# One written-out order of loads and stores on a single DMA queue, with six buffers and equal tiles

## The chip, the cores and the metric

One core of one Trainium2 chip. The metric is the device time of one execution in microseconds (us). "Span" is the length of the profiled execution, some 2 us shorter than the time.

A ratio below is the mean time of one kernel's runs over the mean time of the runs of the kernel before in the same rounds, so it is not quite the ratio of the medians that stand beside it. The batches of runs did not all go to the same chip, and the kernel before had a median between 239.82 and 240.45 us in them; so kernels of different batches are compared by their ratios.

## The reference

```python
# x: (16, 3, 512, 512) float32, factor = 1.5
mean = np.mean(x, axis=(2, 3), keepdims=True)
return np.clip(mean + factor * (x - mean), 0, 1)
```

There are 48 images of 1 MB. Each needs its mean before any of its pixels can be finished. 50.33 MB come in and 50.33 MB go out.

## The kernel before

A tile is four images: 128 partitions of 8192 numbers (32 KB a partition, 4.19 MB), 32 partitions to an image. The last four images are cut into two tiles of two images, whose rows are 16 KB.

```python
TILE_IMGS = [4] * 11 + [2, 2]
X_BUFS = 5
STORE_ENGINE = "gpsimd"
# ... (cut: constants, pools)
for i, N in enumerate(TILE_IMGS):
    # ... (cut: src and dst, rows of 32 KB or 16 KB, contiguous)
    nc.sync.dma_start(out=xt, in_=src)                       # load, SyncE's queue
    nc.vector.tensor_reduce(out=rsum, in_=xt, op=add)        # sums of rows
    nc.tensor.matmul(pbias, blockw[N], rsum)                 # sum over the image's partitions
    nc.scalar.copy(out=bias, in_=pbias)
    nc.scalar.activation(out=xt, in_=xt, func=Relu, bias=bias, scale=factor)
    nc.vector.tensor_scalar(out=xt, in0=xt, scalar1=1.0, op0=min)
    store_eng.dma_start(out=dst, in_=xt)                     # store, GpSimd's queue
```

Of the kernel before, what the change touches and what calls it, by code (L numbers as in the profile page):

```python
# [1 line left out]

# [4 lines left out]


TILE_IMGS = [4] * 11 + [2, 2]  # L10
X_BUFS = 5
STORE_ENGINE = "gpsimd"


@with_exitstack
def kernel(
    ctx: ExitStack,
    tc: tile.TileContext,
    x: bass.AP,
    factor: float,  # L20
    out: bass.AP,
):
    nc = tc.nc
    P = 128

    B, C, H, W = x.shape
    n_img = B * C
    n_pix = H * W

    factor = float(factor)  # L30
    f32 = mybir.dt.float32

    assert sum(TILE_IMGS) == n_img
    NMAX = max(TILE_IMGS)

    x_f = x.rearrange("b c h w -> (b c h w)")
    out_f = out.rearrange("b c h w -> (b c h w)")

    wconst = (1.0 - factor) / float(n_pix)

    consts = ctx.enter_context(tc.tile_pool(name="consts", bufs=1))
    blockw = {}
    for N in sorted(set(TILE_IMGS)):
        wt = consts.tile([P, P], f32, name=f"blockw{N}")
        PPI = P // N
        if N == 1:
            nc.gpsimd.memset(wt, wconst)
        else:
            nc.gpsimd.memset(wt, 0.0)  # L49
            for b in range(N):  # L50
                nc.gpsimd.memset(wt[b * PPI : (b + 1) * PPI, b * PPI : (b + 1) * PPI], wconst)  # L51
        blockw[N] = wt

    xpool = ctx.enter_context(tc.tile_pool(name="xpool", bufs=X_BUFS))
    rpool = ctx.enter_context(tc.tile_pool(name="rpool", bufs=12))
    bpool = ctx.enter_context(tc.tile_pool(name="bpool", bufs=12))
    psum = ctx.enter_context(tc.tile_pool(name="psum", bufs=8, space=bass.MemoryType.PSUM))

    if STORE_ENGINE == "sync":
        store_eng = nc.sync  # L60
    elif STORE_ENGINE == "act":
        store_eng = nc.scalar
    else:
        store_eng = nc.gpsimd

    pix_off = 0
    for i, N in enumerate(TILE_IMGS):
        FREE = n_pix * N // P
        npix_tile = n_pix * N

        xt = xpool.tile([P, NMAX * n_pix // P], f32, name="xt")[:, :FREE]
        src = bass.AP(tensor=x_f.tensor, offset=pix_off, ap=[[FREE, P], [1, FREE]])
        dst = bass.AP(tensor=out_f.tensor, offset=pix_off, ap=[[FREE, P], [1, FREE]])
        nc.sync.dma_start(out=xt, in_=src)  # L74

        rsum = rpool.tile([P, 1], f32)
        nc.vector.tensor_reduce(  # L77
            out=rsum,
            in_=xt,
            axis=mybir.AxisListType.X,  # L80
            op=mybir.AluOpType.add,
        )

        pbias = psum.tile([P, 1], f32)
        nc.tensor.matmul(pbias, blockw[N], rsum, start=True, stop=True)  # L85

        bias = bpool.tile([P, 1], f32)
        nc.scalar.copy(out=bias, in_=pbias)  # L88

        nc.scalar.activation(  # L90
            out=xt,
            in_=xt,
            func=mybir.ActivationFunctionType.Relu,
            bias=bias,
            scale=factor,
        )
        nc.vector.tensor_scalar(  # L97
            out=xt,
            in0=xt,
            scalar1=1.0,  # L100
            scalar2=None,
            op0=mybir.AluOpType.min,
        )
        store_eng.dma_start(out=dst, in_=xt)  # L104

        pix_off += npix_tile


# [1 line left out]
_INS = ['x', 'factor']  # L110
_OUTS = [((16, 3, 512, 512), 'float32')]
#: Inputs that are plain numbers.
_NUMBERS = {'factor': 1.5}


# [26 lines left out]
```

## Time and profile before

| | before |
|---|---|
| time, median | 240.48 us (240.43 to 240.62, 3 runs) |
| span | 238.6 us |
| bytes moved | 100.66 MB |
| VectorE, ScalarE busy | 66%, 37% |

From the page of the kernel before: the busy line, the row of DMA business (tenths, 40 equal slices of the span), the rate in the same slices, and the two queues with their packets, MB and share of the 16 DMA engines' time.

```profile
span 238.6 us, 238 instructions
PE 7.4 (3%) x26; PEld 6.5 (3%) x26; DVE 156.5 (66%) x26; ACT 89.1 (37%) x27; POOL 10.3 (4%) x25
...
DMA  7999999999999999999999999999999999999995
GB/s 269 434 439 439 439 439 352 439 434 439 439 439 439 439 434 434 423 428 412 423 439 439 434 439 439 439 439 439 434 428 426 426 404 428 431 434 439 428 434 214
...
q1 hardware_dynamic: 1872, 50.33, 49.4%
q0 software_dynamic: 1872, 50.33, 49.0%
```

The DMA engines are busy all the time and no computing engine is. Between the first and the last slice the rate is 439 GB/s or close to it, except at the seventh slice (352).

The windows view of the same run gives the rate in stretches of my choice. Its columns are the stretch, its length, the busy time of the five computing engines, the clock, the DMA share and the rate.

```profile
core 0: us, PE busy (x) PEld busy (x) DVE busy (x) ACT busy (x) POOL busy (x), PEclk, DMA share, GB/s
0.00:4.00 4.00, 0.00 (x0) 0.00 (x0) 0.00 (x0) 1.28 (x1) 1.26 (x12) 1.00 0.67 229
4.00:36.00 32.00, 1.14 (x4) 1.00 (x4) 21.96 (x4) 11.16 (x4) 0.00 (x0) 1.00 1.00 430
36.00:42.00 6.00, 0.00 (x0) 0.00 (x0) 6.00 (x1) 3.40 (x1) 0.67 (x1) 1.00 1.01 388
42.00:198.00 156.00, 5.18 (x18) 4.50 (x18) 112.47 (x19) 65.07 (x18) 4.80 (x9) 1.00 1.00 434
198.00:206.00 8.00, 0.56 (x2) 0.50 (x2) 7.66 (x3) 4.35 (x3) 0.69 (x1) 1.00 0.98 414
206.00:232.00 26.00, 0.56 (x2) 0.50 (x2) 8.37 (x3) 3.87 (x2) 2.84 (x3) 1.00 0.99 427
232.00:238.60 6.60, 0.00 (x0) 0.00 (x0) 0.00 (x0) 0.00 (x0) 0.00 (x0) 1.00 0.57 243
```

The view books a packet whole, so short stretches are coarse. The trace also has a record of every packet (start, duration, queue, size). Spread over their durations, these packets give 433 GB/s in the quiet stretches of this trace, loads alone (6 to 30 us), stores alone (210 to 224 us) or a mix; losses below are counted against 433.3. At that rate 100.66 MB need 232.3 us. The span has 6.3 us more: slow first packets (2.6 us lost before 4 us), the end (2.6 us after 232 us), a sag (a short stretch below the full rate, here 0.7 us) at 36 to 42 us, and 0.2 us with the 16 KB rows.

VectorE's two groups in the kernel before (line, engine, operation, operands, count | busy us, mean ns | idle us just before, and what ended it):

```profile
L77 DVE TENSOR_REDUCE rsum<-xt 128x1 f32<-128x8192 f32 (+1 forms) x13 | 104.4, 8029 | 61.7 <-DMA xt<-in_x_dram 61.7
L97 DVE TENSOR_SCALAR xt<-xt 128x8192 f32<-128x8192 f32 (+1 forms) x13 | 53.2, 4091 | 5.0 <-ACT xt L90 5.0
```

VectorE spends its idle time waiting for loads, 61.7 us in all: the computation keeps up.

### The profile page before, as it was taken

To read this page: it belongs to the slowest core of one execution; us is meant where nothing else is said; L and a number is where in the kernel's file an instruction comes from. 1 tells how busy PE (TensorE), PEld (TensorE's weight loads), DVE (VectorE), ACT (ScalarE), POOL (GpSimd) and SP (SyncE) were. 2 spreads that over 40 slices of the span, in tenths; PEclk is the share of its full clock that TensorE was granted. 3 is DMA by queue.
4 is the path that set the end of the run, shared out by engine and by line. 5 is a ranking of instruction groups with operands and counts; after the bars stand their busy time and mean duration, and the time that the engine had idled before them with its cause. 6 is when DMAs were issued, how large, how long until landed. Compare 5 with 4: busy or idle time off the path is not lost.

```text
span 238.6 us, 238 instructions
## 1 busy us (share of the span) xinstructions
PE 7.4 (3%) x26; PEld 6.5 (3%) x26; DVE 156.5 (66%) x26; ACT 89.1 (37%) x27; POOL 10.3 (4%) x25
## 2 busy tenths in 40 slices
PE   0000000000000000000000000000000000000000
PEld 0000000000000000000000000000000000000000
DVE  0088999999599079459629909917945979742300
ACT  2002966472906601900920650470190095406000
POOL 2000001000000000000000000000000000500000
DMA  7999999999999999999999999999999999999995
GB/s 269 434 439 439 439 439 352 439 434 439 439 439 439 439 434 434 423 428 412 423 439 439 434 439 439 439 439 439 434 428 426 426 404 428 431 434 439 428 434 214
DMA packets 3744, 100.66 MB, mean 422 GB/s; under 512 B 416, under 2 KB 416, under 8 KB 416
## 3 DMA queue, kind: packets, MB, share of 16 engines
q1 hardware_dynamic: 1872, 50.33, 49.4%
q0 software_dynamic: 1872, 50.33, 49.0%
HBM read 50.33 MB, written 50.33 MB: 422 GB/s over the span
## 4 chain that ended last, share of the span: by engine, by line
issue 38%; DMA 35%; DVE 18%; POOL 2%; POOLq 0%; SPq 0%
DMA xt<-in_x_dram 19%; DMA out_dram<-xt 16%; DVE rsum L77 11%; DVE xt L97 7%; POOL out_dram L104 2%; POOLq L137 0%; SPq L74 0%; POOLq L104 0%
## 5 line engine op out<-in xcount | busy, mean ns | idle before, releaser
L77 DVE TENSOR_REDUCE rsum<-xt 128x1 f32<-128x8192 f32 (+1 forms) x13 | 104.4, 8029 | 61.7 <-DMA xt<-in_x_dram 61.7
L90 ACT ACTIVATE xt<-xt,bias 128x8192 f32<-128x8192 f32 (+1 forms) x13 | 85.8, 6598 | 0.4
L97 DVE TENSOR_SCALAR xt<-xt 128x8192 f32<-128x8192 f32 (+1 forms) x13 | 53.2, 4091 | 5.0 <-ACT xt L90 5.0
L88 ACT COPY bias<-pbias 128x1 f32<-128x1 f32 x13 | 2.1, 160 | 130.6 <-PE pbias L85 130.6
L104 POOL DMA_DIRECT2D out_dram<-xt x13 | 9.0, 692 | 213.0 <-DVE xt L97 212.8
L85 PE MATMUL pbias<-rsum,blockw 128*128 128x1 f32 x26 | 7.4, 355 | 209.5 <-DVE rsum L77 209.5
L85 PEld LDWEIGHTS pbias<-rsum,blockw 128*128 128x128 f32 x26 | 6.5, 311 | 210.3 <-DVE rsum L77 107.1
L88 ACT ACT_TABLE_LOAD x1 | 1.3, 1283 | 0.8 <-PEq L123 0.8
L51 POOL MEMSET blockw<- 32x32 f32 (+1 forms) x6 | 0.8, 128 | 0.2
L49 POOL MEMSET blockw<- 128x128 f32 x2 | 0.3, 205 | 0.3 <-POOLq L123 0.3
L123 POOL MEMSET const-float32-0.0<- 128x1 f32 x1 | 0.1, 104 | 0.2 <-issue 0.2
L123 POOL MEMSET const-bfloat16-1.0<- 128x1 bf16 x1 | 0.1, 113 | 0.0
L123 POOL MEMSET const-uint8-127<- 128x1 uint8 x1 | 0.1, 113 | 0.0
L123 POOL MEMSET const-float32-1.0<- 128x1 f32 x1 | 0.1, 110 | 0.0
## 6 DMA issues: line engine op xcount, KB each, us to landing
xt<-in_x_dram SPq DMA_DIRECT2D x11, 4096.0 KB, 24.6
out_dram<-xt POOLq DMA_DIRECT2D x11, 4096.0 KB, 36.0
xt<-in_x_dram SPq DMA_DIRECT2D x2, 2048.0 KB, 19.5
out_dram<-xt POOLq DMA_DIRECT2D x2, 2048.0 KB, 19.1
```

The lines of the kernel that those rows point to most:

```text
L49: nc.gpsimd.memset(wt, 0.0)
L51: nc.gpsimd.memset(wt[b * PPI : (b + 1) * PPI, b * PPI : (b + 1) * PPI], wconst)
L77: nc.vector.tensor_reduce(out=rsum, in_=xt, axis=mybir.AxisListType.X, op=mybir.AluOpType.add,)
L85: nc.tensor.matmul(pbias, blockw[N], rsum, start=True, stop=True)
L88: nc.scalar.copy(out=bias, in_=pbias)
L90: nc.scalar.activation(out=xt, in_=xt, func=mybir.ActivationFunctionType.Relu, bias=bias, scale=factor,)
L97: nc.vector.tensor_scalar(out=xt, in0=xt, scalar1=1.0, scalar2=None, op0=mybir.AluOpType.min,)
L104: store_eng.dma_start(out=dst, in_=xt)
L123: nc = _bacc.Bacc("TRN2", target_bir_lowering=False, num_devices=1)
```

## The change

The intent: everything the DMA engines do is put into one queue in an order written out by hand, so that loads and stores take turns evenly; one more buffer; no half tiles. The core of the diff:

```diff
-TILE_IMGS = [4] * 11 + [2, 2]
-X_BUFS = 5
-STORE_ENGINE = "gpsimd"
+P = 128
+ROW = 8192
+BUFS = 6
 # ... (cut)
-    for i, N in enumerate(TILE_IMGS):
-        nc.sync.dma_start(out=xt, in_=src)
-        # ... (the same five operations)
-        store_eng.dma_start(out=dst, in_=xt)
+    def load(t):
+        xt = xpool.tile([P, ROW], f32, name="xt")
+        nc.sync.dma_start(out=xt, in_=dram(x_f, t))
+        tiles[t] = xt
+    def compute(t):
+        # ... (the same five operations)
+    def store(t):
+        nc.sync.dma_start(out=dram(out_f, t), in_=tiles.pop(t))
+    for t in range(min(BUFS, n_tiles)):
+        load(t)
+    for t in range(n_tiles):
+        compute(t)
+        store(t)
+        freed = t - 1
+        if 0 <= freed and freed + BUFS < n_tiles:
+            load(freed + BUFS)
```

On SyncE's queue this gives L0 to L5, S0, S1, L6, S2, L7, S3, L8, S4, L9, S5, L10, S6, L11, S7, S8, S9, S10, S11 (L is a load, S a store, tiles counted from 0).

More of the change, by code (lines that the diff above doesn't have):

```diff
@@ L5 @@
 import concourse.tile as tile
-from concourse import bass_utils, mybir
+from concourse import mybir
 from concourse._compat import with_exitstack
-TILE_IMGS = [4] * 11 + [2, 2]
-X_BUFS = 5
-STORE_ENGINE = "gpsimd"
+P = 128
+ROW = 8192
+BUFS = 6
 @with_exitstack
@@ L23 @@
     nc = tc.nc
-    P = 128
+    f32 = mybir.dt.float32
+    Alu = mybir.AluOpType
+    Act = mybir.ActivationFunctionType
     B, C, H, W = x.shape
-    n_img = B * C
-    n_pix = H * W
+    n_img, n_pix = B * C, H * W
+    ppi = n_pix // ROW
+    per_tile = P // ppi
+    n_tiles = n_img // per_tile
+    assert ppi * ROW == n_pix and per_tile * n_tiles == n_img
     factor = float(factor)
-    f32 = mybir.dt.float32
-    assert sum(TILE_IMGS) == n_img
-    NMAX = max(TILE_IMGS)
+    wconst = (1.0 - factor) / float(n_pix)
@@ L36, with dram @@
     x_f = x.rearrange("b c h w -> (b c h w)")
     out_f = out.rearrange("b c h w -> (b c h w)")
-    wconst = (1.0 - factor) / float(n_pix)
+    def dram(ap, t):
+        return bass.AP(tensor=ap.tensor, offset=t * P * ROW, ap=[[ROW, P], [1, ROW]])
     consts = ctx.enter_context(tc.tile_pool(name="consts", bufs=1))
-    blockw = {}
-    for N in sorted(set(TILE_IMGS)):
-        wt = consts.tile([P, P], f32, name=f"blockw{N}")
-        PPI = P // N
-        if N == 1:
-            nc.gpsimd.memset(wt, wconst)
-        else:
-            nc.gpsimd.memset(wt, 0.0)
-            for b in range(N):
-                nc.gpsimd.memset(wt[b * PPI : (b + 1) * PPI, b * PPI : (b + 1) * PPI], wconst)
-        blockw[N] = wt
@@ L54 @@
-    xpool = ctx.enter_context(tc.tile_pool(name="xpool", bufs=X_BUFS))
-    rpool = ctx.enter_context(tc.tile_pool(name="rpool", bufs=12))
-    bpool = ctx.enter_context(tc.tile_pool(name="bpool", bufs=12))
-    psum = ctx.enter_context(tc.tile_pool(name="psum", bufs=8, space=bass.MemoryType.PSUM))
-    if STORE_ENGINE == "sync":
-        store_eng = nc.sync
-    elif STORE_ENGINE == "act":
-        store_eng = nc.scalar
-    else:
-        store_eng = nc.gpsimd
-    pix_off = 0
-    for i, N in enumerate(TILE_IMGS):
-        FREE = n_pix * N // P
-        npix_tile = n_pix * N
-        xt = xpool.tile([P, NMAX * n_pix // P], f32, name="xt")[:, :FREE]
-        src = bass.AP(tensor=x_f.tensor, offset=pix_off, ap=[[FREE, P], [1, FREE]])
-        dst = bass.AP(tensor=out_f.tensor, offset=pix_off, ap=[[FREE, P], [1, FREE]])
-        nc.sync.dma_start(out=xt, in_=src)
-        rsum = rpool.tile([P, 1], f32)
-        nc.vector.tensor_reduce(
-            out=rsum,
-            in_=xt,
-            axis=mybir.AxisListType.X,
-            op=mybir.AluOpType.add,
-        )
-        pbias = psum.tile([P, 1], f32)
-        nc.tensor.matmul(pbias, blockw[N], rsum, start=True, stop=True)
-        bias = bpool.tile([P, 1], f32)
-        nc.scalar.copy(out=bias, in_=pbias)
-        nc.scalar.activation(
-            out=xt,
-            in_=xt,
-            func=mybir.ActivationFunctionType.Relu,
-            bias=bias,
-            scale=factor,
-        )
-        nc.vector.tensor_scalar(
-            out=xt,
-            in0=xt,
-            scalar1=1.0,
-            scalar2=None,
-            op0=mybir.AluOpType.min,
-        )
-        store_eng.dma_start(out=dst, in_=xt)
-        pix_off += npix_tile
@@ new lines @@
+    xpool = ctx.enter_context(tc.tile_pool(name="xpool", bufs=BUFS))
+    rpool = ctx.enter_context(tc.tile_pool(name="rpool", bufs=2))
+    bpool = ctx.enter_context(tc.tile_pool(name="bpool", bufs=2))
+    psum = ctx.enter_context(tc.tile_pool(name="psum", bufs=2, space=bass.MemoryType.PSUM))
+    blockw = consts.tile([P, P], f32, name="blockw")
+    nc.gpsimd.memset(blockw, 0.0)
+    for a in range(0, P, ppi):
+        nc.gpsimd.memset(blockw[a : a + ppi, a : a + ppi], wconst)
+    tiles = {}
@@ new lines, in load @@
+    def load(t):
[3 more added lines that the diff above has]
+    def compute(t):
+        xt = tiles[t]
+        rsum = rpool.tile([P, 1], f32, name="rsum")
+        nc.vector.tensor_reduce(out=rsum, in_=xt, axis=mybir.AxisListType.X, op=Alu.add)
+        pbias = psum.tile([P, 1], f32, name="pbias")
+        nc.tensor.matmul(pbias, blockw, rsum, start=True, stop=True)
+        bias = bpool.tile([P, 1], f32, name="bias")
+        nc.scalar.copy(out=bias, in_=pbias)
+        nc.scalar.activation(out=xt, in_=xt, func=Act.Relu, bias=bias, scale=factor)
+        nc.vector.tensor_scalar(out=xt, in0=xt, scalar1=1.0, scalar2=None, op0=Alu.min)
```

## The prediction

> **What bounds the kernel.** The data movement. The page gives 100.66 MB in a span of 238.6 us, with the DMA row at 9 tenths in 38 of 40 slices; VectorE is busy 66%, ScalarE 37%. The windows view gives 434 GB/s from 42 to 198 us with loads and stores mixed, and 430 from 4 to 36 us with loads alone; read packet by packet both are 433 GB/s (a 32 KB packet takes 1.213 us on one of 16 engines), and so is the stretch of stores alone (210 to 224 us). The rate does not depend on the mix of directions or the number of queues. The Trainium skill ("DMA: Bandwidth & Descriptors", section "Where 436 GB/s comes from") puts the ceiling at 435 GB/s, and its "Rules for kernel authors" say that spreading DMAs over issuing engines does not help bandwidth; the trace agrees with both.
>
> So the floor is 100.66 MB / 433 GB/s = 232.3 us. The span is 6.3 us above it. From the windows and packets: 0 to 4 us loses 2.6 us (first packet at 1.75 us, slow first packets); 232 to 238.6 us loses 2.6 us (engines finish from 235.1 to 236.8 us, then 1.8 us of completion); 36 to 42 us, at 388 GB/s, loses 0.7 us (the first GpSimd store is issued at 36.06 us, its first packet comes some 4.5 us later, and the load stream sags meanwhile); 198 to 206 us, at 414 GB/s, loses 0.2 us (16 KB rows of the last loads). The rest is noise.
>
> **What the change does.**
> - Stores move from GpSimd's software queue to SyncE's hardware queue: removes the sag, 0.7 us. GpSimd's issue (0.53 us, once 2.46 us) was hidden.
> - Equal tiles remove the 16 KB rows, 0.2 us. The last tile takes 8.7 + 0.6 + 0.2 + 7.1 + 4.4 us to compute, some 22 us, against 11 for a half, but its store has to queue behind others.
> - One FIFO with six buffers: loads 0 to 5 fill it to about 61 us; stores 0 and 1 are ready at 36 and 49 us. Load k waits on SyncE until store k-6 has landed, and holds back what follows. In slots of 9.7 us (4.19 MB at 433 GB/s): loads 0-5, store 0, store 1, load 6, store 2, load 7, ... load 11 in slot 18, stores 7-11 in slots 19-23. When load k is let go, 7 us or more of work is still queued, so the queue never runs dry. Load 11 lands near 187 us, is computed near 210, and its store's turn comes near 225. No compute comes on the path.
> - Reused DMA semaphores (eight in turn) belong to DMAs long done.
>
> Start and end stay.
>
> **Prediction.** 240.5 - 0.9, rounded: 239.5 us, range 238.4 to 240.6. Chances: faster by over 2% 3%, within 2% 94%, slower by over 2% 3%. A gain of 2% would need 4.8 of the 6.3 us above the floor, most of which the change doesn't touch.
>
> **What would show it.** Right: all slices at one rate from 4 us to the end, the slice at 36 us no longer at 352; one hardware queue with about 98% of the engines; SyncE's waits on stores long, yet no gap in the data. Wrong: drops in the GB/s row where loads and stores alternate; a VectorE wait in the chain near the end; the last stores starved.
>
> **What would make it wrong.** In one ring the completion write of a store may hold up the next load (in the tail of stores alone no such gap shows, so I doubt it); the engines may drift apart by more than the present 1.7 us; single-direction blocks may differ from a mix in HBM, which the two pure stretches speak against.

## The result and the profile after

| | before | after |
|---|---|---|
| time, median of 6 runs | 240.45 us (239.74 to 240.75) | 241.63 us (240.99 to 242.50) |
| ratio, 95% interval | | 1.0058 (1.0034 to 1.0083) |
| span of the profiled execution | 238.6 us | 240.7 us |

The kernel became slower by 0.6%: a small loss, clear of the noise, where a gain of 0.4% was predicted. Its runs also spread more, 1.5 us against 1.0. The profiled execution after the change is the slowest of the six (242.50 us), so the second trace below (run a1, 241.56 us) is used beside it.

The page after, the same lines, and the line of the chain that ended last by engine:

```profile
span 240.7 us, 227 instructions
...
DMA  7999999999899999999999999999999999999991
GB/s 272 425 436 436 436 436 436 436 436 430 359 436 436 436 430 430 436 436 436 436 436 430 436 436 436 436 436 430 436 430 436 414 436 430 436 430 430 436 425 71
...
q1 hardware_dynamic: 3456, 100.66, 97.6%
...
DVE 43%; ACT 21%; issue 17%; DMA 9%; PE 2%; SPq 0%; DVEq 0%
```

One queue has 97.6% of the engines' time. The sag did not go: it stands in the eleventh slice (359). The last slice moved only 71 GB/s, against 214 before. The windows view of the changed kernel (columns as before) shows the sag at 58 to 62 us, and the old loss at 198 to 206 us (16 KB rows) gone:

```profile
36.00:58.00 22.00, 0.98 (x4) 0.95 (x4) 22.00 (x4) 10.85 (x3) 0.00 (x0) 1.00 0.99 429
58.00:62.00 4.00, 0.14 (x1) 0.05 (x1) 4.00 (x2) 3.79 (x2) 0.00 (x0) 1.00 1.10 385
62.00:198.00 136.00, 3.90 (x14) 3.50 (x14) 91.82 (x15) 54.45 (x15) 0.00 (x0) 1.00 1.00 431
198.00:206.00 8.00, 0.00 (x0) 0.00 (x0) 8.00 (x2) 0.00 (x0) 0.00 (x0) 1.00 1.04 451
206.00:232.00 26.00, 0.56 (x2) 0.50 (x2) 8.36 (x2) 7.28 (x2) 0.00 (x0) 1.00 0.99 429
```

The end in slices of 1 us, from the windows views (columns as before), of the kernel before and then of the changed one:

```profile
237.00:238.00 1.00, 0.00 (x0) 0.00 (x0) 0.00 (x0) 0.00 (x0) 0.00 (x0) 1.00 0.00 0
238.00:239.00 1.00, 0.00 (x0) 0.00 (x0) 0.00 (x0) 0.00 (x0) 0.00 (x0) 1.00 0.00 0
```

```profile
237.00:238.00 1.00, 0.00 (x0) 0.00 (x0) 0.00 (x0) 0.00 (x0) 0.00 (x0) 1.00 0.08 33
238.00:239.00 1.00, 0.00 (x0) 0.00 (x0) 0.00 (x0) 0.00 (x0) 0.00 (x0) 1.00 0.08 33
```

33 GB/s for 1 us is one packet of 32 KB: after the change a single engine is still at work. How late each engine is, no view says. Every DMA ends with 16 completion writes of 4 bytes, one from each DMA engine, and the trace has a record of each. Those of the last store tell when each engine was done. I took the earliest, the median and the last of these 16, in us from the span's start (my own table, worked out from the packet records):

```
run                      earliest  median    last   last - median   span - last
before                     235.65  235.82  236.82            1.00          1.80
after                      235.59  236.03  239.56            3.53          1.16
a1 (after, again)          236.03  236.53  238.64            2.11          1.15
```

After the change the median engine is 0.2 to 0.7 us later than before, and the last engine 1.8 to 2.7 us later. In the first trace after it is one single engine that works alone for 3 us at its own speed; 15 engines were done by 236.5 us. The end after the last packet is 0.6 us shorter.

The kernel before has late engines too: four of them end at 236.7 to 236.8 us, 1 us after the median. By the packet records three of these fell 0.75 us behind the median engine at 196 to 206 us, beside the 16 KB rows of the last loads, and the fourth 0.8 us before 44 us. The 0.2 us that the 16 KB rows cost as a mean over 16 engines was thus more on the engines that ended last.

Where does the late engine lose its time? In a saturated stretch a packet starts where the packet before it on the same engine ended, so the records can be chained into 16 engines. The usual 32 KB packet takes 1.213 us. In the trace after, every engine's packet 47 (counted from 0: the last row of L5, the load ahead of S0) takes 1.65 to 1.9 us, and on eleven engines packet 46 takes 1.3 us or more as well: that is the sag. Later the packets of 1.3 us or more are single ones, at 89 to 90, 109 to 110, 128, 148 to 149, 170 and 186 to 187 us: in the main the last row of a load that is followed by a store. No last row of a store ahead of a load is among them. On the late engine four of them come sooner in its list; its packet of 2.33 us at 128 us is the next-to-last row of L8, its packet of 1.90 us at 187 us the third from the last of L11. That of 2.33 us starts at 128.40 us, as does another engine's slow last row of L8 (1.35 us). Late engines of a1 and a3 below show the same (next-to-last rows of L10 and L11 at 166 to 167 and at 187 us). So the slow packets go with the time at which the engines turn, and an engine that is already late loses again; why, no run tells.

The page alone leads elsewhere. It names VectorE for 43% of the chain that ended last, and its groups have changed:

```profile
L67 DVE TENSOR_REDUCE rsum<-xt 128x1 f32<-128x8192 f32 x12 | 104.2, 8680 | 14.2 <-DMA xt<-in_x_dram 14.2
L73 DVE TENSOR_SCALAR xt<-xt 128x8192 f32<-128x8192 f32 x12 | 53.1, 4423 | 52.3 <-ACT xt L72 52.3
```

VectorE now waits 52.3 us for ScalarE (5.0 before) and only 14.2 us for loads. From tile 6 on each tile goes alone through sum, activation and minimum, 21.1 us a tile, while the data need 19.4 us a tile (two times 4.19 MB at 433 GB/s). The last minimum (timeline, changed kernel) starts at 218.02 us:

```profile
218.02 4.43 DVE L73 TENSOR_SCALAR xt<-xt 128x8192 f32<-128x8192 f32 x1 [8.08 <-ACT xt L72]
```

It ends at 222.45 us, and its store is issued at once. The prediction had that tile ready near 210 us. The first engines finish the store ahead of it at 225.9 us, so 3.4 us of slack were left: a near miss, but the engines' records show no gap in the data. SyncE's waits (the DMA queue's own view) are long and harmless for the same reason:

```profile
SPq L61 <- DMA out_dram<-xt: 107.6, 6, 23.1
SPq L76 <- DVE xt L73: 103.5, 5, 32.2
```

### The profile page after: what moved, and what is told of

Its sections match the earlier page's. It is cut to its first block, busy times and chain, and to the rows that moved or that the text cites. A ratio compares the mean times of both kernels' runs of the same rounds, so it can differ in the third digit from the quotient of the medians.

```text
span 240.7 us, 227 instructions
## 1 busy us (share of the span) xinstructions
PE 6.7 (3%) x24; PEld 6.0 (2%) x24; DVE 156.0 (65%) x24; ACT 88.7 (37%) x25; POOL 0.9 (0%) x9
## 3 DMA queue, kind: packets, MB, share of 16 engines
q1 hardware_dynamic: 3456, 100.66, 97.6%
## 4 chain that ended last, share of the span: by engine, by line
DVE 43%; ACT 21%; issue 17%; DMA 9%; PE 2%; SPq 0%; DVEq 0%
DVE rsum L67 35%; ACT xt L72 21%; DMA xt<-in_x_dram 9%; DVE xt L73 8%; PE pbias L69 2%; ACT bias L71 0%; SPq L61 0%; DVEq L73 0%
## 5 line engine op out<-in xcount | busy, mean ns | idle before, releaser
L67 DVE TENSOR_REDUCE rsum<-xt 128x1 f32<-128x8192 f32 x12 | 104.2, 8680 | 14.2 <-DMA xt<-in_x_dram 14.2
L73 DVE TENSOR_SCALAR xt<-xt 128x8192 f32<-128x8192 f32 x12 | 53.1, 4423 | 52.3 <-ACT xt L72 52.3
L72 ACT ACTIVATE xt<-xt,bias 128x8192 f32<-128x8192 f32 x12 | 85.5, 7122 | 0.4
L69 PE MATMUL pbias<-rsum,blockw 128*128 128x1 f32 x24 | 6.7, 349 | 203.9 <-DVE rsum L67 203.9
L69 PEld LDWEIGHTS pbias<-rsum,blockw 128*128 128x128 f32 x24 | 6.0, 311 | 204.5 <-issue 195.4
L55 POOL MEMSET blockw<- 32x32 f32 x4 | 0.5, 118 | 0.2
```

The costliest lines, as they stand in the source:

```text
L55: nc.gpsimd.memset(blockw[a : a + ppi, a : a + ppi], wconst)
L67: nc.vector.tensor_reduce(out=rsum, in_=xt, axis=mybir.AxisListType.X, op=Alu.add)
L69: nc.tensor.matmul(pbias, blockw, rsum, start=True, stop=True)
L72: nc.scalar.activation(out=xt, in_=xt, func=Act.Relu, bias=bias, scale=factor)
L73: nc.vector.tensor_scalar(out=xt, in0=xt, scalar1=1.0, scalar2=None, op0=Alu.min)
```

## The experiments

I call "ring" the list of one queue's packets that one DMA engine works off, and "turn" a place in it where a load is followed by a store. Theory 1: each turn inside the one queue delays single engines, and since nothing evens the engines out, the delays add up to a late last engine. Rivals: an accident of one execution; the equal tiles or the sixth buffer; VectorE's chain; hardware queues for stores as such.

### a1: the changed kernel again

No edit.

> The changed kernel once more, for a second trace. In its first trace 15 of the 16 DMA engines end within 0.9 us (235.6 to 236.5 us) and one ends at 239.6 us. Theory (turns in one ring): each turn from load to store in the one queue costs some engine up to about 1 us, and it piles up on whichever engine is unlucky: again one or two engines end 1.5 to 3.5 us after the median engine, time 241 to 242.5. Rival (an accident of that one execution, or noise): the engines end within 1.5 us of each other and the time is 239.5 to 240.5.

Measured: 241.42 us, ratio 1.0049 (1.0021 to 1.0077). Four engines end after 237.3 us, at 237.4, 238.1, 238.6 and 238.6; the median is 236.5. So it is not an accident, and it is not always one engine: the delays fall differently in each execution. That fits the wider spread of the times.

### a2: the stores back on GpSimd's queue

```diff
-        nc.sync.dma_start(out=dram(out_f, t), in_=tiles.pop(t))
+        nc.gpsimd.dma_start(out=dram(out_f, t), in_=tiles.pop(t))
```

> The changed kernel with its stores back on GpSimd's queue; six buffers and equal tiles kept. Theory (turns in one ring): no straggling engine, all ends within 1.5 us, the sag of 0.7 us at the first store stays because it belongs to the first store and not to the queue: 239.8 to 240.5 us. Rival 1 (the equal last tiles or the sixth buffer cost the time): stays at 241 to 242. Rival 2 (the sag is GpSimd's): the changed kernel's sag at 58 to 61 us disappears or moves only here.

Measured: 239.69 us, ratio 0.9978 (0.9950 to 1.0007): 1.7 us under a1 in the same rounds, a little under what was expected. The profiled run is the fastest of the six (239.13 us). All 16 engines end between 235.42 and 235.72 us. Rival 1 falls: six buffers and equal tiles cost nothing. The rate of a2 by slices, from its page:

```profile
span 237.4 us, 231 instructions
...
GB/s 265 442 442 442 442 442 353 442 442 442 442 442 425 420 414 420 442 442 442 442 442 442 442 420 409 409 442 442 442 442 442 442 442 425 409 403 442 442 442 265
```

The sag is in the seventh slice again (353), at the first store.

### a3 and a4: no computation, one queue or two

Both leave out `compute` (wrong results). a4 also has

```diff
-        nc.sync.dma_start(out=dram(out_f, t), in_=tiles.pop(t))
+        nc.scalar.dma_start(out=dram(out_f, t), in_=tiles.pop(t))
```

> Wrong on purpose: the changed kernel with no computation, only its loads and stores in their order on SyncE's queue. Theory (turns in one ring): the straggling engine is there without any computation, last engine 1.5 us or more after the median one, time 240.5 to 242. Rival (VectorE's chain of 21 us per tile, which the page names as 43% of the chain that ended last): with no computation the time falls clearly, below 239.

> Wrong on purpose: as a3, but the stores go out from ScalarE's hardware queue. Theory (turns in one ring): the two rings are served in turn, packet by packet, and no engine straggles: last engine within 1.3 us of the median, 0.8 to 2 us faster than a3. Rival (hardware queues for stores are what costs, whichever engine issues): same straggler and the same time as a3.

Measured: a3 241.69 us, ratio 1.0062 (1.0032 to 1.0092); a4 239.21 us, 0.9959 (0.9929 to 0.9988), 2.5 us faster than a3 and so by more than expected. The windows view of the end of a3 and then of a4 (with no computing engine but GpSimd in it; the last two columns are share and rate):

```profile
core 0: us, POOL busy (x), PEclk, DMA share, GB/s
232.00:236.00 4.00, 0.00 (x0) 1.00 0.95 410
236.00:240.00 4.00, 0.00 (x0) 1.00 0.12 49
```

```profile
232.00:236.00 4.00, 0.00 (x0) 1.00 0.91 393
236.00:240.00 4.00, 0.00 (x0) 1.00 0.00 0
```

In a3 there are still 12% of the engines' time busy from 236 to 240 us (last engine at 238.60, median 236.52); in a4 nothing (all between 235.84 and 236.23). With no computation at all the time is that of the changed kernel: VectorE's chain, though the page names it, had no part in the loss. And two hardware queues, one for each direction, don't lose: it is not the hardware queue for stores. In a4 the sag comes at 16 to 20 us, where its first stores start.

### b1: fewer turns in the one queue

```diff
-        freed = t - 1
-        if 0 <= freed and freed + BUFS < n_tiles:
-            load(freed + BUFS)
+        if t % 2 == 1:
+            for f in (t - 1, t):
+                if f + BUFS < n_tiles:
+                    load(f + BUFS)
```

> The changed kernel, still one queue, with the steady part in pairs (two stores, two loads, two stores ...): 4 turns from load to store instead of 7. Theory (each turn in the one ring costs the worst engine some 0.4 to 0.5 us: last engines at 238.6 to 239.6 us with 7 turns, 235.7 with two rings): last engine at about 237.2 us, time about 240.0 to 240.6, some 1.0 to 1.5 us under the changed kernel's 241.4. Rival (one ring costs as such, whatever the order): 241.4 as before.

Measured: 239.89 us, ratio 0.9997 (0.9971 to 1.0023); last engine at 237.15 us, median 236.06. Three turns less give back some 0.55% (1.0049 and 1.0058 against 0.9997), and the time lies just under the expected range.

### b2 and b3: the same halves, 7 or 13 turns

Every load and store is cut into two halves of the columns, on SyncE's queue. The order of the steady part:

```diff
 # b2                          # b3
 store(t, 0)                   store(t, 0)
-store(t, 1)                  +load(t + 5, 0)
-load(t + 5, 0)               +store(t, 1)
 load(t + 5, 1)                load(t + 5, 1)
```

> Control for b3: every load and store cut into two halves of the columns (16 KB rows), one queue, order as in the changed kernel (both halves of a store, then both of a load): still 7 turns. Theory and rival alike: the 16 KB rows cost some (0.611 us for 16 KB against 1.213 for 32 KB in the trace of before: about 1.7 us in all), so 242 to 244 us, with the same spread of the engines' ends as the changed kernel.

> The same halves as b2, in the order half store, half load, half store, half load: 13 turns from load to store. Theory (cost per turn): the worst engine is 2 to 3 us later than in b2, time 1.5 to 3 us above b2. Rival (cost per byte or per DMA, not per turn): same time as b2 within 0.5 us.

Measured: b2 241.95 us, ratio 1.0093 (1.0052 to 1.0134); b3 243.53 us, 1.0155 (1.0127 to 1.0183). Last engine minus median: 1.90 us in b2, 3.81 us in b3. Same packets, same bytes, same number of DMAs: six turns more cost 1.58 us by the medians (1.48 by the means), at the low end of what was expected. b2 itself lies just under its expected range. The intervals of the two ratios touch, since b2's four runs spread over 1.6 us, but all four runs of b3 (243.44 us and up) lie above all four of b2 (243.08 and below). The rival (a cost per DMA or per byte) falls.

### b4 and c2: is the sag a cold start of the first writes?

Both are a2 with one more store at the start, which the right one overwrites later: 64 KB (from `blockw`, into the last tile's place) in b4, 1 MB of zeros (into the first tile's place) in c2.

```diff
+    nc.gpsimd.dma_start(
+        out=bass.AP(tensor=out_f.tensor, offset=(n_tiles - 1) * P * ROW, ap=[[ROW, P], [1, P]]),
+        in_=blockw)                                                             # b4
+    nc.gpsimd.dma_start(
+        out=bass.AP(tensor=out_f.tensor, offset=0, ap=[[ROW, P], [1, 2048]]), in_=early)   # c2
```

> a2 (stores on GpSimd's queue, six buffers, equal tiles) with one extra store of 64 KB into the last tile's place at the start, overwritten later. Theory (the sag of 0.7 us at the first store is a cold start of the first writes to memory): the sag at 38 us is gone or below 0.2 us, the time falls by 0.4 to 0.8 us under a2's, to about 239.0. Rival (the sag comes from the first change-over under a full load queue): the sag stays at 38 us, time equal to a2's or a little longer.

> a2 (stores on GpSimd's queue) with one extra store of 1 MB of zeros (8 KB rows) into the first tile's place at the start, overwritten later. The extra bytes cost 1.05 MB / 433 GB/s = 2.4 us. If the sag at 38 us is a cold start that enough early writing takes away (the 64 KB of b4 being too little, or in another place), the sag at 38 us is gone and the time is a2's + 1.7, about 241.4. If the sag belongs to the moment when a stream of stores joins a stream of loads, the sag stays at 38 us and the time is a2's + 2.4 or more, 242 and up.

Measured: b4 239.75 us, ratio 0.9996 (0.9971 to 1.0021), nothing gained over a2, and its sag is there in full: 0.83 us lost from 36 to 44 us (packet records against 433.3 GB/s). c2 241.88 us, 1.0079 (1.0056 to 1.0102): by the ratios, which hold across batches, a2 + 2.4 us, the full cost of the extra bytes (by the medians a2 + 2.2, between the two expectations). In c2 0.52 us are lost from 4 to 14 us, where the early store runs, and 0.19 us at 36 to 46 us: the sag has moved, and its sum is about what it was (0.50 us in a2, 0.73 in the kernel before). So 64 KB early take nothing away, 1 MB early moves most of it, and no time was won. What the sag is stays open.

### c1: two queues that each carry both directions

```diff
+    def ring(t):
+        return nc.sync if t % 2 == 0 else nc.scalar
-        nc.sync.dma_start(out=xt, in_=dram(x_f, t))
+        ring(t).dma_start(out=xt, in_=dram(x_f, t))       # the store likewise
```

No computation, as a3 and a4.

> Wrong on purpose (no computation): two hardware queues as in a4, but each carries loads and stores: even tiles on SyncE's, odd tiles on ScalarE's, 4 turns from load to store in each. Theory as it stands (a turn costs only where a ring is served alone; a second ring fills it): no straggler, last engine within 1.3 us of the median, 239.0 to 239.6 us as a4. Rival (loads and stores have to be kept in separate rings, a turn costs in any ring): last engine 1.5 us or more after the median, 240 us or more.

Measured: 243.78 us, ratio 1.0167 (1.0137 to 1.0197), the slowest of the copies; engines end between 237.2 and 240.4 us. The theory "as it stands" in that expectation falls: a second ring does not fill the turn.

I took it that both rings went from loads to stores together; d1's expectation below says so. The compiled order is another: SyncE's queue has L0 L2 L4 S0 L6 S2 ..., and ScalarE's L1 L3 S1 L5 S3 L7 ..., so from 42 to 200 us one ring loads while the other stores, and at about 61, 80, 100, 120, 140, 160 and 180 us they swap. The windows view of c1 around two swaps:

```profile
core 0: us, POOL busy (x), PEclk, DMA share, GB/s
44.00:60.00 16.00, 0.00 (x0) 1.00 0.99 426
60.00:66.00 6.00, 0.00 (x0) 1.00 1.04 415
66.00:80.00 14.00, 0.00 (x0) 1.00 1.03 445
80.00:84.00 4.00, 0.00 (x0) 1.00 0.91 311
84.00:100.00 16.00, 0.00 (x0) 1.00 1.02 442
```

The traffic of the core is a mix all through, between 170 and 260 GB/s from each queue by the packet records (in stretches of 4 us), and yet at the swap at 80 us the rate falls to 311 GB/s. By the packet records the swaps at 61, 80, 120 and 160 us cost 0.53, 0.78, 0.82 and 0.64 us, those at 100, 140 and 180 us under 0.1 us each. From 80 us on it is thus every second swap that costs: those in which ScalarE's ring goes from loads to stores and SyncE's back to loads, and not the opposite ones. At 61 us an opposite one cost time, so this is no rule yet.

### d1: two mixed queues, half a beat apart

The orders written out, with six fixed buffers, no computation:

```diff
+    even = "L0 L2 S0 L4 S2 L6 S4 L8 S6 L10 S8 S10".split()      # SyncE's queue
+    odd = "L1 L3 L5 S1 L7 S3 L9 S5 L11 S7 S9 S11".split()       # ScalarE's queue
```

> Wrong on purpose (no computation). As c1, two hardware queues that each carry loads and stores, but half a beat apart: in every slot of the middle one queue loads while the other stores, so each ring still turns from load to store (5 times each), back to back, while the traffic of the whole core stays a mix. Theory A (what costs is the switch of the whole core's traffic from loads to stores, as in the one queue and in c1, where both rings turned together): no straggler, last engine within 1.3 us of the median, no sag after the first, 239.0 to 240.0 us. Theory B (a turn inside any one ring costs): as c1, last engine 1.5 us or more after the median, 241.5 us or more.

Measured: 241.86 us, ratio 1.0071 (1.0045 to 1.0097); engines end between 236.8 and 238.8 us. (ScalarE's queue has four turns, not five.) The time is theory B's; the last engine, 1.3 us after the median one, is theory A's. The time went mostly in two further sags in which all engines lost alike, 0.74 us at 84 to 90 us and 0.88 us at 103 to 108 us. And the run is not as clean as it was meant: the beat held only to about 80 us; then ScalarE's queue stood empty from 82 to 86 us, and the two queues loaded together and stored together at times. So d1 alone decides nothing. Theory A, that only a switch of the whole core's traffic costs, is refuted by c1 read rightly: there the core's traffic never switched, and four of the seven swaps cost time all the same, whether from load to store or back can't be told, for the two rings swap at once. Not every turn costs: in d1 ScalarE's turn at 61 us cost nothing measurable.

### c3 and d2: a right kernel with a queue for each direction

c3 is the changed kernel with `nc.scalar.dma_start` for the stores.

> The changed kernel with its stores on ScalarE's hardware queue, correct results. Theory (two rings; the hardware queue's end after the last packet was 1.2 us in the one-queue traces against 1.7 to 1.8 us with GpSimd's): no straggler, 238.9 to 239.5 us, a little under a2. Rival (the waits of the stores on ScalarE hold up its activations until the stores run late): gaps in the data or a late last store, 240 or more.

Measured: 246.01 us, ratio 1.0253 (1.0226 to 1.0280): slower, as the rival had it. The waits of ScalarE in c3 (us in total, times, longest), and the windows view (columns as before):

```profile
ACT bias L71 <- DVE xt L73: 70.4, 3, 37.7
ACT xt L72 <- DVE xt L73: 36.2, 2, 31.2
```

```profile
170.00:178.00 8.00, 0.00 (x0) 0.00 (x0) 8.00 (x2) 0.00 (x0) 0.00 (x0) 1.00 0.93 401
178.00:182.00 4.00, 0.56 (x2) 0.50 (x2) 4.00 (x1) 0.00 (x0) 0.00 (x0) 1.00 0.00 0
182.00:190.00 8.00, 0.00 (x0) 0.00 (x0) 8.00 (x3) 0.00 (x0) 0.00 (x0) 1.00 0.92 393
```

A store waits at the head of ScalarE's stream for VectorE's minimum, and the activations behind it wait too, up to 37.7 us. From 178 to 182 us there was no data to move: all loads were in, and the next store was issued only at 182.30 us.

d2 keeps the two queues and writes the order out:

```diff
+    with tc.manual_schedule():          # every engine in the order written
+        for t in range(min(BUFS, n_tiles)):
+            load(t)
+        front(0)                        # sum, matmul, copy, activation
+        for t in range(n_tiles - 2):
+            front(t + 1)
+            back(t)                     # minimum, store on ScalarE's queue, load(t + BUFS)
+        back(n_tiles - 2)
+        front(n_tiles - 1)
+        back(n_tiles - 1)
```

> Correct results. Stores on ScalarE's hardware queue as in c3, but VectorE and ScalarE in a written-out order: the sum of tile t+1 before the minimum of tile t, the store of tile t after the activation of tile t+1, so that no store waits long at the head of ScalarE's queue. Theory (c3 was slow by ScalarE's waits at stores that held up activations, 37.7 us at the longest, and by a gap in the data near 180 us, not by hardware stores): no gap, no straggler, 238.8 to 239.5 us. Rival (hardware stores beside hardware loads are slower once there is computation): 241 or more without a gap in the data.

Measured: right results, 239.12 us, ratio 0.9952 (0.9934 to 0.9971). Its page:

```profile
span 237.1 us, 223 instructions
...
GB/s 265 442 442 442 442 437 359 442 442 442 431 415 415 420 442 442 442 442 442 442 426 415 409 431 442 442 442 442 442 437 420 420 415 431 442 442 442 442 442 265
...
q1 hardware_dynamic: 1728, 50.33, 49.8%
q10 hardware_dynamic: 1728, 50.33, 49.2%
```

All engines end between 235.50 and 235.91 us, and the end after the last packet is 1.15 us, as with one hardware queue. The sag at the first store is still there (359). d2 is faster than both kernels: by 0.5% than the kernel before, by about 1% than the changed one (1.0058 over 0.9952).

### All runs together

```
run     rings, what they carry          turns in a ring   ratio    last engine, us
before  2, one direction each           0                 1        236.8
a2      2, one direction each           0                 0.9978   235.7
a4      2, one direction each (copy)    0                 0.9959   236.2
d2      2, one direction each           0                 0.9952   235.9
b1      1, both                         4                 0.9997   237.2
after   1, both                         7                 1.0058   239.6
a1      1, both                         7                 1.0049   238.6
a3      1, both (copy)                  7                 1.0062   238.6
b2      1, both, 16 KB rows             7                 1.0093   239.1
b3      1, both, 16 KB rows             13                1.0155   240.9
d1      2, both in each (copy)          5 and 4           1.0071   238.8
c1      2, both in each (copy)          4 and 5           1.0167   240.4
```

(The ratio is that of all runs of a kernel, the last engine that of its one trace. b4 and c2 carry extra stores and c3 a gap; they are left out.)

## Why the prediction was wrong

- **What bounds the kernel: right.** The rate of 433 GB/s, and with it the floor of 232.3 us, hold in the quiet stretches with 32 KB rows (430 with the 16 KB rows of b2 and b3). The Trainium skill ("DMA: Bandwidth & Descriptors", "Where 436 GB/s comes from") gives a fabric ceiling of 435 GB/s, with which this agrees. The same section says that for transfers between HBM and SBUF the HBM side, about 358 GB/s, binds; these transfers ran at 433, so here the measurement decides.
- **"Stores move ... to SyncE's hardware queue: removes the sag, 0.7 us": wrong.** The sag belongs to the first stores, not to GpSimd. It was 0.73 us before, 0.87 and 0.68 us after, 0.67 us with stores on ScalarE's queue (d2). The delay from the first store's issue to its first packet, which I had read as GpSimd's, is there with a hardware queue too: 4.7 us before (36.06 to 40.72), 4.9 us in d2 (35.72 to 40.66). Two things that happened together were taken for cause and effect.
- **"Equal tiles remove the 16 KB rows, 0.2 us": right for the rate, mis-sized for the end.** The loss at 198 to 206 us is gone. But 0.2 us was a mean over 16 engines; three of the four engines that ended last before had lost some 0.75 us there. What that is worth in time isn't shown: a2 is 0.5 us faster than the kernel before (0.9978), within its noise.
- **"The rate does not depend on the mix of directions or the number of queues", and so "start and end stay": true of stretches, false of turns.** This is the step that failed and decides the sign. The steady rates are equal, but a ring that changes direction loses time on some engines, and nothing makes it up. The last engine ended 1.8 to 2.7 us later than before, where the prediction had it 0.9 us earlier. b1, b2 and b3 show that it goes with the number of turns, a3 that it needs no computation, a2, a4 and d2 that it goes away with a ring for each direction.
- **"The engines may drift apart by more than the present 1.7 us": named rightly, but not weighed.** It stood among the things that would make the prediction wrong and had no share in the range. It is what happened: 4.0 us from the first engine to the last in the first trace after, 2.6 us in the second. (By the completion writes it had been 1.2 us before, not 1.7.)
- **"The completion write of a store may hold up the next load": not this.** In the trace after, the slow packets are those of a load with a store behind it.
- **"No compute comes on the path": right, barely.** The last tile was ready at 222.45 us rather than near 210, because VectorE and ScalarE fell into taking turns; 3.4 us of slack were left.
- **Not foreseen, and a gain:** the end after the last packet is 1.15 to 1.33 us in the traces with hardware queues alone (1.16 after), against 1.64 to 1.80 us in those with GpSimd's (1.80 before).

The sum, from the first trace after: last packet 2.74 us later (239.56 against 236.82), end 0.64 us shorter, together 2.1 us of span. That trace is of the slowest of six runs; in a1 it is 1.82 us later and 0.65 us shorter, together 1.2 us, which is also the difference of the median times.

What stays open: what in a ring makes the turn cost time, why in the one queue single engines lose most and others little, why some turns are free (d1 at 61 us, c1 at 100, 140 and 180 us), and what the sag at the first stores is. No run here tells these apart.

## What to carry to other kernels

Give loads and stores a queue each when the DMA engines are the bound; if they must share one, let it change direction seldom. When all 16 DMA engines look busy to the end, look at when each of them finishes, since a kernel ends with its last engine and the mean hides it. If the stores' queue belongs to a computing engine, write that engine's order out so that no store waits at its head (c3 against d2: 3% between the same transfers).

## What the Trainium skill lacked or had wrong

- "DMA: Bandwidth & Descriptors", "Rules for kernel authors", says that spreading DMAs over SP, ACT and GpSimd does not help bandwidth and only saves issue time. The steady rate agrees (433 GB/s with one queue or two), but one queue for each direction was about 1% faster than one queue for both (a4 against a3: 0.9959 against 1.0062), and no issue time was saved: in a3 no engine stood idle for more than 0.11 us between two packets from 4 to 235 us.
- The same page, "Queues, rings and completion order", says that each engine goes round its rings packet by packet; the mixed stretches of the two-queue runs agree (170 to 260 GB/s from each queue in c1, and in the chained records 99.9% of the packets of an engine between 70 and 180 us follow one of the other queue, 85 to 88% in the kernel before, a2, a4 and d2). It says nothing of a cost when one ring changes direction: by estimate 0.26 us of the kernel's time for each turn from load to store from b3 minus b2 (1.58 us for six), 0.45 us from the changed kernel against b1 (0.56% for three), and some turns in c1 and d1 nothing measurable.
- The same page, "Latency and other measured facts", says that DMA engines 7 and 15 are usually slower and suspects the software queue. Here one run with the software queue (a2) had all engines done within 0.3 us, another (the kernel before) had four engines 1 us late, and the latest engines, up to 3.8 us, came with one hardware queue; the records carry no engine number, so which engine it was can't be told.
- I found no page that mentions the sag at the first stores: 0.5 to 1.0 us at full rate in the runs that were measured for it (0.73 before, 0.87 after, 0.50 in a2, 0.99 in a4; in c2, with the early store, 0.52 at that store and 0.19 at the usual place).
